# Seven block products in place of eight: six pairs of the first feed forward, nine pairs of the MLP

## The chip, the cores and the metric

The kernel runs on one core of a Trainium2 chip. The metric is the device time of one execution in microseconds (us); several runs are made and their median is taken. Beside the times there is one profiled execution, whose rows are shown below.

The engines are TensorE (PE in the rows; its weight loads are PEld), VectorE (DVE), ScalarE (ACT), GpSimd (POOL) and SyncE (SP), which issues the DMAs. Each of them works through its own queue in order. TensorE writes its results to PSUM, which holds eight banks of 128 x 512 float32 numbers; all other tiles lie in SBUF.

## What is computed

Two transformer blocks in a row on one sequence of 256 tokens with 1024 features, in float32. The first block has a mixer of three attention branches, an attention to a memory, and a gated feed forward; the second has modulation rows computed from a vector `c`, a mixer of forgetting attention and retention, and an MLP. The two parts that the change touches, cut to their core:

```python
# first block: D_FF = 2816
a = u @ w_in                                        # 1024 -> 2 * D_FF
h = h + (silu(a[..., :D_FF]) * a[..., D_FF:]) @ w_out
# second block: D_FF_2 = 4096
u = square(relu(h @ w_mlp_in))
x = x + gate_f * (u @ w_mlp_out)
```

## The kernel before

**Operands in two parts.** Each float32 operand is split into a high part that TensorE takes as fp32r and a low part, the rest. `mm3` makes one product out of three matmuls: high by high, low by high, high by low. The weights are split as they are used: a DMA brings a tile `raw` of 128 x 1024, ScalarE copies it into the high part `wh`, VectorE subtracts to get the low part `wl` (`cols`).

**A planner writes the order.** `Plan` records every operation; a list scheduler then gives each engine its order and each tile its slot before anything runs. An operation's key is its latest start by the planner's own costs, or its earliest start plus a margin (8 us in most entries) if that comes first. Among operations that can start, the smaller key goes first. `TUNING` holds one entry of parameters for each 140 dense matmuls (`WINDOW`) in the order they are issued, some with extra leads for named chains. The dense matmuls themselves keep the order of the program. SBUF tiles come from pools of slots: 37 of 4 KB (`k4`), 14 of 2 KB (`k2`), 12 of 1 KB; PSUM has eight slots (`ps`). A DMA may be placed up to 30 us (`HORIZON`) ahead of its need, if a slot is free.

**The first feed forward (`swiglu`, `ffn`).** The hidden width is cut into 11 pairs of 128 rows. For each pair, `up` makes two products with transposed output (`dense_T`): `aa` for the silu half and `bb` for the other, 48 matmuls of 256 columns each, one PSUM bank each. `glu` applies silu on ScalarE, multiplies on VectorE, and splits the product into the pair's hidden tile `hT`. `out_steps` multiplies `hT` by the rows of `w_ffn_out` into five accumulators (`out_accs`: two of 512 columns for token tile 0; 512, 256 and 256 for tile 1), which stay in PSUM for the whole stage. So three banks are left for `up`. The last six steps (`LAG1`) are done for token tile 0 first and then for tile 1, so that the norm of tile 0 starts early. `between` starts parts of the modulation: each part is four DMAs of `w_ada_2` tiles and four multiply-and-sum instructions on VectorE (`mod_part`); `MODF` lists the pairs after which one is started.

**The MLP (`mlp`).** 16 pairs, the last two (`TAIL`) plain as above. For the other 14 a pair's product with `w_mlp_out` is a 2 x 2 block product: two token tiles by two row blocks, and two row blocks by two halves of 512 columns. Plain, that is eight block products of three matmuls, 24 matmuls of 512 columns. For the pairs listed in `FASTM` a scheme with seven block products (`FAST`) is used: 21 matmuls, and in exchange sums of blocks, made on VectorE: of the activations in `pair_sums`, of the weights in `pair_weights`. The results are kept as seven accumulators in seven PSUM banks for the whole stage, plain pairs (`PLAIN`) adding into the same seven; `pair_end` combines them at the end and adds them to `x`. One bank is left for `up`. A pair's product is made two pairs after its `up`.

Of the kernel before, what the change touches and what calls it, by code (L numbers as in the profile page):

```python
# [15 lines left out]
AF = mybir.ActivationFunctionType  # L16
ALU = mybir.AluOpType
# [3 lines left out]
P = 128  # L21
S = 256
NT = 2
DM = 1024
KT = 8
D_FF = 2816
# [78 lines left out]
FFN = [2] * 11  # L105
# [531 lines left out]
class Net:  # L637
# [1012 lines left out]
    def swiglu(self, u, done):  # L1650
        nc, flow = self.nc, self.flow
        mods = []

        def swi(t, ac):
            sl = self.k(1, [P, S], nm="silu")
            nc.scalar.activation(sl, ac[:, :S], AF.Silu)
            yield
            nc.vector.tensor_tensor(sl, ac[:, S:], sl, ALU.mult)
            yield
            return sl  # L1660

        def glu(hT, aa, bb, n):
            sl = self.k(2, [P, n, S], nm="silu")
            nc.scalar.activation(sl, aa, AF.Silu)
            yield
            nc.vector.tensor_tensor(sl, bb, sl, ALU.mult)
            yield
            self.split(hT[0][0], hT[1][0], sl)
            yield

        def up(k0, n):
            hT = self.hidden(n)
            if k0 == 0:
                return hT, self.first_up(hT, u, n, [("w_ffn_in", 0), ("w_ffn_in", D_FF)], swi)
            aa, = self.dense_T(u, self.cols("w_ffn_in", k0 * P, (k0 + n) * P), n * P)
            bb, = self.dense_T(u, self.cols("w_ffn_in", D_FF + k0 * P, D_FF + (k0 + n) * P), n * P)
            return hT, [flow.start(glu(hT, aa, bb, n), "glu")]

        def between(i):
            if i in MODF:  # L1680
                self.next_part()
            if i == 9:
                self.scale, self.shift, self.gain = self.mod(1), self.mod(0), self.gain_row(self.a["norm_final"])

        self.ffn("ffn", FFN, "w_ffn_out", up, done, LAG1, between)


    def modulation(self):
# [525 lines left out]
        self.out_steps(self.out_accs(), [(hT, k, 2 * tail + k) for k in range(2 * TAIL)], w_out, True, done, 3)  # L2214

LAG1, LAG2 = 6, 6
TAIL, FASTM = 2, (2, 4, 6, 8, 10, 12, 13)
MODF = (0, 2, 4, 5, 6, 7)
MODG = ((4, 0), (4, 1), (1, 0), (5, 0))


def build(tc, a, out):
    with ExitStack() as ctx:
        e = ctx.enter_context
        n = Net(a)
        nc, flow = n.flow, n.flow
        x = n.fixed(NT * DM, "x").rearrange("p (t n) -> p t n", t=NT)
        for t in range(NT):
            nc.lead = LEADS[3 + t]
            for c in range(0, DM, 512):  # L2230
                nc.sync.dma_start(x[:, t, c:c + 512], a["x"][t * P:(t + 1) * P, c:c + 512])
        nc.lead = 0.0
        n.setup()
        u, mem = n.mixer(x)
        u = n.memory_attention(x, u, mem)
        late = {}

        def end_ffn(t, acs):
            if t == 0:
                late["u"] = n.act_pair()  # L2240
                late["chain"] = n.block2_norm(x, late["u"], n.gain)
            n.norms[t] = flow.start(late["chain"](t, acs), "b2norm")

        n.swiglu(u, end_ffn)

        def end_mix(t, acs):
            if t == 0:
                late["u2"] = n.act_pair()
            n.norms[t] = flow.start(n.resume(x, t, acs, late["u2"], (n.scale2, n.shift2), n.gate), "mlpnorm")

        n.block2_mix(x, late["u"], end_mix)
        n.x = x
        ends = []

        def end(t, acs):
            ends.append(flow.start(n.resume(x, t, acs, gate=n.gate, store=out)))

        n.mlp(late["u2"], end)
        flow.need(*ends)
        flow.need(*flow.waiting)  # L2260
        flow.schedule()
        wk, ps = e(tc.tile_pool(name="wk", bufs=1)), e(tc.tile_pool(name="ps", bufs=1, space=PSUM))
        dram = e(tc.tile_pool(name="dram", bufs=1, space=bass.MemoryType.DRAM))

        def place(r):
            if r.kind == "ps":
                return ps.tile([P, 512], F32, tag=f"ps{r.slot}", name=r.name)
            if r.kind == "dram":
                return dram.tile([P, r.n], r.dtype, name=r.name)
            return wk.tile([P, r.n], r.dtype, tag=r.name if r.kind == "fixed" else f"{r.kind}_{r.slot}", name=r.name)  # L2270

        flow.issue(tc, place)
# [42 lines left out]
```

## Time and profile before

| | us |
|---|---|
| median of 3 runs (757.82 to 758.5) | 757.98 |
| the profiled execution | 758.92 |
| its span, first to last instruction | 757.1 |
| TensorE busy in the span | 740.1 (98%) |
| VectorE busy | 611.9 (81%) |
| ScalarE busy | 420.3 (56%) |

The busy time of TensorE counts matmuls with modelled ends, which overlap; how fast it works is read from the starts of the matmuls in the timeline. Rows name tiles by the program's names without their numbers; nearly all operations are issued through one helper, so that their line is L634.

### The profile page before, as it was taken

The numbers are of one execution on the slowest core, as the hardware profiler recorded it, in microseconds if no ns is written. First come the engines' busy times: TensorE is split into PE (matmuls) and PEld (weight loads), VectorE is DVE, ScalarE is ACT, GpSimd is POOL, SyncE is SP. The second block draws the span as 40 slices with busy tenths as digits, with TensorE's granted clock in tenths as the row PEclk, the third lists the DMA queues.
The fourth block names the chain that finished last, engine by engine and source line by source line (L and its number), as shares of the span: only waits on it lengthen the run. The fifth ranks groups of instructions, "written<-read, shape, count | busy, mean of one in ns | idle before, by whom it ended". The sixth has DMA issues, their size and how long they took to land.

```text
span 757.1 us, 13129 instructions
## 1 busy us (share of the span) xinstructions
PE 740.1 (98%) x5090; PEld 671.9 (89%) x5090; DVE 611.9 (81%) x1026; ACT 420.3 (56%) x701; POOL 39.9 (5%) x50
## 2 busy tenths in 40 slices
PE   7999999999998999999999899999999999999998
PEld 4978999999897999999999788898887989998996
DVE  5999989798699995877455788888669879898857
ACT  6684875456287644344354555753546746767640
POOL 0012000010000000000000222020101000000000
PEclk9999999999999999999999999999999999999999
DMA  9828476976375797888877476545455487755521
GB/s 316 287 85 256 144 249 234 389 275 214 129 268 182 237 313 232 310 308 299 279 266 182 147 162 155 150 120 186 164 166 170 137 271 267 268 193 196 196 84 56
DMA packets 94931, 161.69 MB, mean 214 GB/s; under 512 B 8011, under 2 KB 58347, under 8 KB 94868
## 3 DMA queue, kind: packets, MB, share of 16 engines
q1 hardware_dynamic: 94868, 160.85, 65.3%
q8 instruction: 40, 0.66, 0.4%
q14 instruction: 23, 0.19, 0.1%
HBM read 159.75 MB, written 1.08 MB: 212 GB/s over the span
## 4 chain that ended last, share of the span: by engine, by line
PE 74%; DVE 13%; issue 6%; ACT 3%; DMA 3%; POOL 1%; SPq 0%; POOLq 0%; DVEq 0%; ACTq 0%
PE ps L634 74%; DVE wl L634 3%; DMA raw<-in_w_in_dram 2%; DVE x L634 1%; DVE s L634 1%; DVE xn L634 1%; DVE sc L634 1%; ACT wh L634 1%; DVE sum L634 1%; DVE gt L634 0%; SPq L634 0%; POOL s L634 0%; DVE mk L634 0%; DMA row<-in_norm_mix_dram 0%; ACT prob L634 0%
## 5 line engine op out<-in xcount | busy, mean ns | idle before, releaser
L634 DVE TENSOR_TENSOR wl<-raw,wh 128x1024 fp32r<-128x1024 f32 (+4 forms) x237 | 278.6, 1204 | 42.0 <-ACT wh L634 34.1
L634 PE MATMUL ps<-aT,wh 128*128 128x256 f32 x1664 | 305.8, 283 | 0.0
L634 ACT ACTIVATE wh<-raw 128x1024 fp32r<-128x1024 f32 (+4 forms) x237 | 241.9, 1040 | 106.3 <-DMA raw<-in_w_ffn_in_dram 24.2
L634 PEld LDWEIGHTS ps<-aT,wh 128*128 128x128 f32 x1664 | 258.4, 189 | 1.9 <-issue 0.4
L634 PE MATMUL ps<-aT,wl 128*128 128x256 f32 x832 | 235.9, 284 | 0.0
L634 PE MATMUL ps<-wh,aT 128*128 128x512 f32 (+5 forms) x672 | 182.2, 357 | 2.1 <-ACT wh L634 1.3
L634 PEld LDWEIGHTS ps<-aT,wl 128*128 128x128 f32 x832 | 157.1, 189 | 0.1
L634 PEld LDWEIGHTS ps<-wh,aT 128*128 128x128 f32 x672 | 118.8, 190 | 19.1 <-ACT wh L634 1.9
L634 PE MATMUL ps<-wl,aT 128*128 128x512 f32 (+5 forms) x336 | 117.5, 354 | 0.0
L634 PEld LDWEIGHTS ps<-wl,aT 128*128 128x128 f32 x336 | 63.6, 190 | 7.1
L634 PE MATMUL ps<-wh,hT 128*128 128x512 f32 (+1 forms) x260 | 67.6, 348 | 0.0
L634 DVE SCALAR_TENSOR_TENSOR raw<-raw,mod_c 128x1024 f32<-128x1024 f32 x48 | 57.3, 1219 | 8.0 <-DMA raw<-in_w_ada_dram 7.8
L634 PEld LDWEIGHTS ps<-wh,hT 128*128 128x128 f32 x260 | 45.3, 188 | 6.9
L634 PE MATMUL ps<-wl,hT 128*128 128x512 f32 (+1 forms) x130 | 45.2, 348 | 0.0
L634 PE MATMUL ps<-wh,blockl 128*128 128x512 f32 x105 | 41.4, 394 | 0.0
L634 PE MATMUL ps<-wh,blockh 128*128 128x512 f32 x105 | 41.4, 394 | 0.0
L634 PE MATMUL ps<-wl,blockh 128*128 128x512 f32 x105 | 41.4, 394 | 0.0
L634 POOL TENSOR_TENSOR s<-s,mhalf 128x1 f32<-128x1 f32 (+3 forms) x22 | 23.5, 1072 | 298.0 <-DVE s L634 297.8
L634 ACT ACTIVATE junk<-x 128x512 f32<-128x512 f32 (+1 forms) x29 | 16.1, 555 | 38.7 <-DVE x L634 36.4
L634 PEld LDWEIGHTS ps<-wl,hT 128*128 128x128 f32 x130 | 24.5, 188 | 3.4
L634 ACT ACTIVATE prob<-ps,s 128x256 f32<-128x256 f32 (+1 forms) x48 | 20.0, 447 | 9.4 <-DVE s L634 9.3
L634 ACT ACTIVATE aT<-ps 128x256 fp32r<-128x256 f32 (+1 forms) x41 | 17.7, 459 | 11.1 <-PE ps L634 10.7
(300 smaller groups left out, 807.2 us busy)
## 6 DMA issues: line engine op xcount, KB each, us to landing
raw<-in_w_in_dram SPq DMA_DIRECT2D x62, 512.0 KB, 6.0
raw<-in_w_ada_dram SPq DMA_DIRECT2D x48, 512.0 KB, 6.0
raw<-in_w_ffn_in_dram SPq DMA_DIRECT2D x44, 512.0 KB, 5.9
raw<-in_w_mlp_in_dram SPq DMA_DIRECT2D x32, 512.0 KB, 4.2
raw<-in_w_mlp_out_dram SPq DMA_DIRECT2D x32, 512.0 KB, 5.3
raw<-in_w_ffn_out_dram SPq DMA_DIRECT2D x22, 512.0 KB, 5.2
raw<-in_w_out_dram SPq DMA_DIRECT2D x16, 512.0 KB, 4.5
raw<-in_w_up_dram SPq DMA_DIRECT2D x6, 512.0 KB, 5.3
```

The lines of the kernel that those rows point to most:

```text
L634: getattr(get[o.eng], name)(*map(real, args), **{k: real(v) for k, v in kw.items()})
```

## The change

The first feed forward gets the structure of the MLP. `ps` are seven accumulators. Pairs 2 to 7 use the seven products, pairs 0 and 1 the eight, and the last three pairs (`TAILF`) are plain, through `out_steps`. A pair's product comes two pairs after its `up` (`LATE`), and is cut in two: four block products stand between the two halves of the next `up`, the other three or four behind it. The silu product is now written into a page of blocks. The modulation parts are started after pairs 3 to 8 in place of 0, 2, 4, 5, 6 and 7. In the MLP, pairs 3 and 9 join `FASTM`. `n.x = x` only moves up, since `pair_end` is now used earlier. The diff, cut to its core:

```diff
-        def glu(hT, aa, bb, n):
-            sl = self.k(2, [P, n, S], nm="silu")
-            nc.scalar.activation(sl, aa, AF.Silu)
-            yield
-            nc.vector.tensor_tensor(sl, bb, sl, ALU.mult)
-            yield
-            self.split(hT[0][0], hT[1][0], sl)
-            yield
-
-        def up(k0, n):
-            hT = self.hidden(n)
-            if k0 == 0:
-                return hT, self.first_up(hT, u, n, [("w_ffn_in", 0), ("w_ffn_in", D_FF)], swi)
-            aa, = self.dense_T(u, self.cols("w_ffn_in", k0 * P, (k0 + n) * P), n * P)
-            bb, = self.dense_T(u, self.cols("w_ffn_in", D_FF + k0 * P, D_FF + (k0 + n) * P), n * P)
-            return hT, [flow.start(glu(hT, aa, bb, n), "glu")]
+        x, w_in, w_out, n = self.x, "w_ffn_in", "w_ffn_out", D_FF // S
+        tail = n - TAILF
+        blocks, pages, chains = {}, {}, {}
+        hT, ps = self.act_pair(), [self.acc() for _ in range(7)]
+
+        def first(t, ac):
+
+            o = yield from swi(t, ac)
+            pt, = yield from self.bank()
+            for j in range(2):
+                self.tr(pt[:, j * P:(j + 1) * P], o[:, j * P:(j + 1) * P])
+            self.pair_place(pages[0], pt[:, :S], t)
+            yield
+
+        def sums(p, *before):
+            yield from flow.after({0: list(before)})
+            blocks[p] = yield from self.pair_sums(pages[p], p in FASTF)
+
+        def silu(p, sl, ac):
+            nc.scalar.activation(sl, ac, AF.Silu)
+            yield
+
+        def glu(p, sl, ac):
+            yield from flow.after({0: chains["a", p]})
+            if p >= tail:
+                nc.vector.tensor_tensor(sl, ac, sl, ALU.mult)
+                yield
+                c, k = divmod(2 * (p - tail), 4)
+                self.split(*(e[c][:, k:k + 2, :] for e in hT), sl)
+                yield
+                return
+            pages[p] = self.pair_page()
+            flat = "p a b -> p (a b)"
+            nc.vector.tensor_tensor(pages[p][:, 0:4, :].rearrange(flat), ac.rearrange(flat), sl.rearrange(flat), ALU.mult)
+            yield
+            yield from sums(p)
+
+        def up(p, part, fn, sl):
+            c0 = part * D_FF + p * S
+            ac, = self.dense_T(u, self.cols(w_in, c0, c0 + S), S)
+            chains["ab"[part], p] = flow.start(fn(p, sl, ac), "glu")
+
+        begun = set()
+
+        def down(p, which, w):
+            flow.need(chains["b", p])
+            self.pair_product(ps, blocks[p], w, begun, p == tail - 1, which)
...
-        self.ffn("ffn", FFN, "w_ffn_out", up, done, LAG1, between)
+        self.main("ffn")
+        pages[0] = self.pair_page()
+        wf = [self.held(w_in, c, c + S) for c in (0, D_FF)]
+        firsts = []
+        for t in range(NT):
+            flow.need(self.norms[t])
+            ac = self.acc()
+            for i in range(2):
+                self.dense_t(u, t, wf[i], ac[:, i * S:(i + 1) * S])
+            firsts.append(flow.start(first(t, ac), f"first_{t}"))
+        chains["b", 0] = flow.start(sums(0, *firsts), "glu")
+        between(0)
+        for p in range(1, n + LATE):
+            sl = self.k(2, [P, 2, S], nm="silu")
+            q = p - LATE
+            w = self.pair_weights(w_out, 2 * q, q in FASTF) if 0 <= q < tail else None
+            if p < n:
+                self.main("ffn")
+                up(p, 0, silu, sl)
+            if w:
+                down(q, slice(0, 4), w)
+            if p < n:
+                up(p, 1, glu, sl)
+            if w:
+                down(q, slice(4, 8), w)
+            if p < n:
+                between(p)
+        flow.need(flow.start(self.pair_end(ps, x), "ffnsum"))
+        flow.need(*[chains["b", p] for p in range(tail, n)])
+        self.out_steps(self.out_accs(), [(hT, k, 2 * tail + k) for k in range(2 * TAILF)], w_out, True, done, LAG1)
...
-TAIL, FASTM = 2, (2, 4, 6, 8, 10, 12, 13)
-MODF = (0, 2, 4, 5, 6, 7)
+TAIL, TAILF, LATE, FASTF, FASTM = 2, 3, 2, (2, 3, 4, 5, 6, 7), (2, 3, 4, 6, 8, 9, 10, 12, 13)
+MODF = (3, 4, 5, 6, 7, 8)
```

## Rows read from the trace of the kernel before

**Rows 1.** The chain that ended last, feed forward and MLP: start us, us, what.

```profile
243.60 181.42 PE ps L634 x1345
...
576.97 164.67 PE ps L634 x1045
```

**Rows 2.** Busy us by engine in four stretches, then granted clock, DMA share, GB/s.

```profile
243.60:425.00 181.40, 181.40 (x1347) 172.77 (x1348) 125.51 (x153) 80.40 (x95) 1.16 (x2) 1.00 0.80 260
577.00:741.70 164.70, 164.70 (x1046) 148.54 (x1047) 137.86 (x196) 104.60 (x142) 0.00 (x0) 1.00 0.58 198
632.00:648.00 16.00, 16.00 (x109) 14.72 (x108) 15.72 (x27) 8.53 (x13) 0.00 (x0) 1.00 0.94 328
424.00:440.00 16.00, 14.02 (x77) 11.07 (x76) 14.60 (x32) 11.57 (x25) 4.00 (x4) 0.89 0.56 167
```

**Rows 3.** Timeline of TensorE, matmuls of 256 and 512 columns: start us, us.

```profile
305.31 0.40 PE L634 MATMUL ps<-aT,wh 128*128 128x256 f32 x2
...
316.24 0.39 PE L634 MATMUL ps<-aT,wh 128*128 128x256 f32 x2
...
726.69 0.40 PE L634 MATMUL ps<-wh,blockh 128*128 128x512 f32 x1
...
729.49 0.39 PE L634 MATMUL ps<-wh,blockh 128*128 128x512 f32 x1
```

**Rows 4.** Groups of VectorE in the feed forward (248 to 424 us) by shape.

```profile
L634 DVE TENSOR_TENSOR wl<-raw,wh 128x1024 fp32r<-128x1024 f32 x62 | 75.2, 1222 | 32.2 <-ACT wh L634 24.6 <-PE ps L634 6.8
L634 DVE SCALAR_TENSOR_TENSOR raw<-raw,mod_c 128x1024 f32<-128x1024 f32 x24 | 28.7, 1218 | 2.3 <-DMA raw<-in_w_ada_dram 2.2
```

**Rows 5.** Groups of VectorE in the MLP (584 to 736 us) by shape.

```profile
L634 DVE TENSOR_TENSOR sums<-raw,raw 128x512 f32<-128x512 f32 x14 | 9.6, 688 | 2.7 <-DMA raw<-in_w_mlp_out_dram 2.5
L634 DVE TENSOR_TENSOR wl<-sums,wh 128x1024 fp32r<-128x1024 f32 x7 | 8.5, 1217 | 0.0
L634 DVE TENSOR_TENSOR blocks<-blocks 128x128 f32<-128x128 f32 x28 | 6.8, 283 | 0.1
...
L634 DVE TENSOR_TENSOR blockl<-blocks,blockh 128x384 fp32r<-128x384 f32 x7 | 3.8, 549 | 0.0
```

**Rows 6.** Timeline of VectorE, instructions that follow on one another.

```profile
257.99 4.62 DVE L634 TENSOR_TENSOR wl<-raw,wh 128x1024 fp32r<-128x1024 f32 x4
...
741.09 0.68 DVE L634 TENSOR_TENSOR sum<-sum,modrow 128x512 f32<-128x512 f32 x1
741.69 0.68 DVE L634 TENSOR_TENSOR sum<-ps,sum 128x512 f32<-128x512 f32 x1
```

**Rows 7.** Timeline of TensorE, the last matmul of two `bb` banks.

```profile
299.63 0.28 PE L634 MATMUL ps<-aT,wl 128*128 128x256 f32 x1
...
384.02 0.28 PE L634 MATMUL ps<-aT,wl 128*128 128x256 f32 x1
```

**Rows 8.** Timeline of VectorE, the products that empty these two banks.

```profile
299.95 0.69 DVE L634 TENSOR_TENSOR silu<-ps,silu 128x512 f32<-128x512 f32 x1 [2.90 <-PE ps L634]
...
386.84 0.68 DVE L634 TENSOR_TENSOR silu<-ps,silu 128x512 f32<-128x512 f32 x1
```

**Rows 9.** Timeline of ScalarE: a late silu of the feed forward, a late relu.

```profile
381.87 0.58 ACT L634 ACTIVATE silu<-ps 128x512 f32<-128x512 f32 x1
...
728.90 0.58 ACT L634 ACTIVATE relu<-ps 128x512 f32<-128x512 f32 x1
```

**Rows 10.** Instructions by tile: the weight DMAs' first and last start, their landing, last uses.

```profile
L634 SPq DMA_DIRECT2D raw<-in_w_ffn_in_dram x44: 367/378/1089, 203.9 to 378.7; - x44
...
L634 DVE TENSOR_TENSOR silu<-ps,silu x12: 414/692/692, 250.1 to 412.6; 128x512 f32<-128x512 f32 x10, 128x256 f32<-128x256 f32 x2
...
L634 SPq DMA_DIRECT2D raw<-in_w_mlp_in_dram x32: 367/379/660, 542.5 to 707.9; - x32
...
DMA to landing us min/median/max: 3.3/4.2/8.9
...
L634 ACT ACTIVATE relu<-ps x16: 569/598/602, 585.4 to 737.5; 128x512 f32<-128x512 f32 x16
```

More of the change, by code (lines that the diff above doesn't have):

```diff
@@ L2232, in build @@
         nc.lead = 0.0
+        n.x = x
         n.setup()
@@ L2251, in build @@
         n.block2_mix(x, late["u"], end_mix)
-        n.x = x
         ends = []
```

## The prediction

> **What bounds the kernel now.** I read the chain that ended last first. In both stages that change it is TensorE alone: one unbroken piece of 1345 matmuls over 181.4 us of the feed forward and one of 1045 over 164.7 us of the MLP [rows 1]. The reader is to see that no other engine has a link in either piece: there time goes only if TensorE has less to do, and comes back only if something makes it wait. [...] The timeline of TensorE gives its pace by starts: 93 matmuls of 256 columns in 10.93 us, 0.1175 us each, and 12 of 512 in 2.80 us, 0.233 us each [rows 3]. (The durations in the rows overlap and are no pace.)
>
> **What the change removes.** A pair with seven block products has 21 matmuls for 24: 3 x 0.233 = 0.70 us. Six pairs of the feed forward and two more of the MLP: 8 x 0.70 = 5.6 us. In the feed forward the eight block pairs also lose the cut of token tile 1 into 512, 256 and 256 columns: six times 2 x 0.1175 - 0.233 = 0.002 us a pair, 0.1 us in all. So 5.7 us of TensorE, 4.3 of them in the feed forward. All of it is on the path, since nothing else is in the chain.
>
> **What it adds on VectorE.** A turn of the loop in the middle (turns 4 to 9, with a fast pair and a modulation part each) holds: four splits of up weights, two of down weights, four weight sums of 512, the splits of the two sum tiles (1024 and 512), four block sums of 128, block splits of 512 and 384, the silu product of 512, and four modulation sums of 1024. Instructions that follow on one another start closer than their durations: four of 1024 in 4.62 us, 1.155 us each, against 1.222 in the group; those of 512 start 0.60 us apart against 0.68 [rows 4, 6]. The lag between two is hidden by about 0.07 to 0.08, so I put 384 at 0.47 and 128 at 0.20 (groups: 0.549 and 0.283) [rows 5]. The turn: 4.62 + 2.31 + 2.40 + 1.76 + 0.80 + 1.07 + 0.60 + 4.62 = 18.2 us. TensorE needs 96 x 0.1175 + 21 x 0.233 = 16.2 us. VectorE is therefore the slower engine in these six turns, by 2.0 us each, 12 us in all.
>
> What hides that is the lead with which weights are fetched. The last up tile of the MLP is issued at 707.9 and used by the last 24 matmuls before the relu at 737.5, from 734.4 on: 26.5 us; less landing (4.2 us) and the two split instructions, about 20 us of finished work. In the feed forward the last one leads by some 31 us (378.7; used 2.8 us before 412.6) [rows 10]. After the change the feed forward holds tiles as the MLP does now (pages and blocks of up to three pairs, six to eight weight pages for a fast pair), so I take the MLP's 20 us. 12 is less than 20, turns 1 to 3 are light, and the MLP stretch at 98% [rows 2] did not stop TensorE: cost nothing, bounds nothing to 2 us (durations in place of starts: 19.9 us a turn, 22 us in six turns, 2 more than 20). If the cover is gone, each turn costs its whole excess of 2.0 to 3.7 us. In the MLP two more pairs become fast, some 4.7 us of VectorE each; 137.9 + 9.4 = 147 of 163 us, still covered.
>
> [...]
>
> **What it adds in PSUM.** The feed forward had five accumulators and three banks for `up`; now seven and one. Each of the two products of an `up` must be emptied while the block products behind it run: 12 matmuls, 2.8 us, behind the silu half; nine, 2.1 us, behind the other half of a fast pair. From the start of the last matmul into the bank that leaves 2.9 and 2.2 us. Behind a bank that is late stands the whole queue of TensorE.
>
> How late is it today, with nothing hanging on it? The second half is mostly emptied at once: last matmul at 299.63, VectorE's product ends at 300.64, 1.0 us. So in nine of ten pairs; once it took 3.5 us (384.02 to 387.52, behind a split) [rows 7, 8]. The first half is looser: going back 48 matmuls from 384.02, its last one started at 378.4, and the silu ended at 382.45, 4.1 us later [rows 7, 9]. Over pairs 2 to 10 I find about 0.9 us five times, and 2.1, 2.6, 3.5 and 4.1. The MLP empties its one bank by a relu in 0.7 to 1.4 us twelve times and in 2.8 to 2.9 us three times of 15, as at 728.90 (ends 2.8 us after the pair's products began at 726.69) [rows 3, 9]; behind it stand 4.9 us of products, so it never showed.
>
> With 0.25 us for TensorE to notice (an estimate from the 0.32 us between 299.63 and VectorE's start at 299.95 [rows 7, 8]): first half, 3.5 and 4.1 would stop TensorE 0.8 and 1.4 us, 0.25 us a pair; by the MLP's relu 0.04; I take 0.2. Second half: 3.5 stops it 1.55 us in one of ten, 0.16 a pair. Eight pairs: 8 x 0.36 = 2.9 us. Bounds: nothing, if the planner, which knows the eight slots, empties them in time as in the MLP; 8 x (1.4 + 1.55) = 24 us if every bank is as late as the worst. I take 2.9 since most are prompt.
>
> **What it moves.** `pair_end` is eleven VectorE instructions, 11 x 0.60 = 6.6 us [rows 6], behind the last block product. Turn 10 follows with 96 matmuls, 11.3 us, and needs one bank at once and a second 5.6 us later, when the first of the seven is long free: cost nothing; without that turn, up to 6.6 us. The tail of three plain pairs with the two token tiles one after the other is as before. The modulation parts move past the first pairs; their rows are needed after the stage, their DMAs are the same 24, and SP issues nothing new: nothing. The planner's entries count matmuls: 66 fewer in the feed forward shift all later entries by half a window, so the leads for the projections behind it fall on other operations. The nearest row is that transition, where TensorE is idle 2.0 of 16 us [rows 2]: from 2 us gained to 2 us lost; I take nothing.
>
> **Sum.** -5.7 + 2.9 = -2.8 us. The profiled execution took 758.9 us, so 756.1; the median of the runs stands 0.9 us below it: 755.2 us, faster by 0.4%. About 0.2%, 1.5 us, is what a measurement here can tell from no change.
>
> **The rivals.**
> *The whole saving arrives* (752.3 us). For it: the MLP with one spare bank and a nearly full VectorE shows no pause. Against: its products behind a bank last 4.9 us, here 2.8 and 2.1.
> *One bank is too few* (757 to 759.4 us, the same). If hand-overs cost twice what I take, 5.8 us, the saving is gone. For it: VectorE has less slack in these turns than when the one late product in ten was counted. It decides from 0.5 us a pair on. [...]
> *VectorE becomes the bound* (slower). Its groups waited 32 us before 62 splits, about 0.5 us each [rows 4]; if six splits a turn keep that wait while VectorE is behind, a turn takes 18.2 + 3.1 = 21.3 us, 5.1 over TensorE's; six turns are 31 us, 11 beyond the lead of 20. -5.7 + 2.9 + 11 = +8, 766 us. It decides from 16.2 + 20 / 6 = 19.5 us a turn on. Against: most of that wait was for work not yet there, and the 98% stretch [rows 2] has next to none.
> *The later stages lose by the shifted entries* (2 us lost, with 4.5 us of hand-overs: 758.8; 4 us lost: 760.8).
>
> **How the numbers follow.** My forecast, 753.5 to 756.4 us, 0.42; the whole saving, 751 to 753.5, 0.20; one bank too few, 756.5 to 759.5, 0.18; VectorE the bound, 0.12; later stages lose beyond the bound, 0.08. Faster 0.62, same 0.18, slower 0.20. The likeliest case's own range is 753.5 to 756.4. The range that leaves two in ten out is 751.6 to 760.0: the whole saving with a little from the shift at one end, mild forms of the slower cases at the other.
>
> **What would show it.** Right: the feed forward's piece of TensorE about 177 to 180 us long with a few gaps under 1.6 us, each behind a silu or its product; starts still 0.1175 and 0.233 us apart; the MLP's piece 1.4 us shorter without gaps; VectorE near 95% in the middle of the feed forward. Wrong: gaps in TensorE's weight loads that end with `wl`, growing from turn 4 to 9 (VectorE the bound); gaps of a microsecond at every hand-over (one bank too few); both pieces shorter by their full share and the time not (the stages behind).

## The result and the profile after

| | before | after |
|---|---|---|
| median of 4 runs each, us | 758.10 (757.82 to 758.50) | 753.66 (752.07 to 754.89) |
| ratio, 95% interval | | 0.9939 [0.9927, 0.9952] |
| the profiled execution, us | 758.92 | 754.89 |
| its span, us | 757.1 | 753.1 |

The change makes the kernel 4.4 us (0.6%) faster. The forecast was 755.2; the measured time lies at the lower edge of the likeliest case (753.5 to 756.4). The profiled executions of the kernel after, of e6 and of e9 are the slowest among the runs of each (754.89, 759.65 and 762.40 us).

The chain that ended last, of the kernel after, answers to [rows 1]: start us, us, what.

```profile
375.79 12.11 DMA raw<-in_w_ffn_in_dram
387.98 1.06 ACT wh L634
389.04 0.49 ACT silu L634
389.57 31.93 PE ps L634 x207
...
424.08 2.23 DVE wl L634
427.10 0.90 DVE xn L634
...
574.67 162.95 PE ps L634 x1039
```

The MLP is still one piece of TensorE, 1.7 us shorter. The feed forward is no longer one: the chain enters TensorE at 389.57 from a silu, that from a weight split on ScalarE, and that from a DMA that took 12.11 us. And where the feed forward ends, the chain now passes through VectorE (`wl`, then `xn`).

The feed forward and the MLP as in [rows 2], and two stretches from the middle of the feed forward, of the kernel after: us; busy us of PE, PEld, DVE, ACT, POOL; granted clock, DMA share, GB/s.

```profile
243.20:424.70 181.50, 180.27 (x1308) 169.94 (x1308) 165.22 (x238) 93.99 (x122) 2.43 (x3) 1.00 0.78 263
574.70:737.60 162.90, 162.90 (x1040) 146.91 (x1041) 146.75 (x213) 107.81 (x146) 0.00 (x0) 1.00 0.58 200
...
320.00:360.00 40.00, 40.00 (x290) 37.63 (x289) 39.83 (x61) 21.60 (x26) 0.00 (x0) 1.00 0.88 296
360.00:390.00 30.00, 28.77 (x203) 26.60 (x203) 29.97 (x43) 15.27 (x20) 0.00 (x0) 1.00 0.93 332
```

VectorE went from 125.5 to 165.2 us in the feed forward and is busy 99.6% and 99.9% of two stretches in a row; TensorE still paused only once there. The engine at 99.9% is not what it paused for, as the timelines of TensorE and ScalarE show around that pause:

```profile
387.71 0.40 PE L634 MATMUL ps<-wh,blockl 128*128 128x512 f32 x1
387.94 0.40 PE L634 MATMUL ps<-wl,blockh 128*128 128x512 f32 x1
389.57 0.50 PE L634 MATMUL ps<-aT,wh 128*128 128x256 f32 x2 [1.23 <-ACT silu L634]
```
```profile
386.47 1.06 ACT L634 ACTIVATE wh<-raw 128x1024 fp32r<-128x1024 f32 x1 [5.63 <-DMA raw<-in_w_ffn_in_dram]
387.98 1.06 ACT L634 ACTIVATE wh<-raw 128x1024 fp32r<-128x1024 f32 x1 [0.45 <-DMA raw<-in_w_ffn_in_dram]
388.94 0.58 ACT L634 ACTIVATE silu<-ps 128x512 f32<-128x512 f32 x1
```

The silu empties the one spare bank. It stands in ScalarE's queue behind two weight splits, the first of which waited 5.63 us for its tile. TensorE starts 1.4 us later than its pace of 0.23 us would have had it. A place like this, where a bank is emptied while block products run and TensorE then goes on with the next half of an `up`, is a hand-over. The stage has 16, and the other 15 came in time: at 14 of them the silu or the product ended 0.9 to 1.6 us after the start of the bank's last matmul, and at the last, where the product ended 3.8 us after it, TensorE had already gone on in another bank.

Only eleven of the 16 test a single spare bank. The eight plain block products (`PLAIN`) add into four accumulators, not into all seven as the description of the kernel says, and the planner gives a tile its bank at its first use. The other three accumulators take theirs in the first half of pair 2's product, so the four hand-overs before that had banks to spare; the last one had accumulators that were already read out. e6 below shows the second spare bank.

The group of these splits in the kernel after, and the landing of the up weights, beside 5.9 us median and 9.4 at most before:

```profile
L634 ACT ACTIVATE wh<-raw 128x1024 fp32r<-128x1024 f32 x58 | 60.4, 1054 | 30.6 <-DMA raw<-in_w_ffn_in_dram 13.7 <-PE ps L634 6.5 <-DVE raw L634 5.3
```
```profile
DMA to landing us min/median/max: 3.5/7.0/12.1
```

Where the 4.0 us of the two spans went, from the starts of matmuls in the two timelines. FFN is the feed forward's first to last matmul, the gap that from there to the first matmul of the next projection (proj2); the MLP is counted up to its last block product, and 15.2 us follow in both kernels:

| us | before the FFN | FFN | gap | proj2 to MLP | MLP |
|---|---|---|---|---|---|
| before | 243.80 | 185.18 | 1.42 | 144.28 | 167.25 |
| after | 243.24 | 182.22 | 3.07 | 143.82 | 165.56 |
| difference | -0.56 | -2.96 | +1.65 | -0.46 | -1.69 |

So -4.3 + 1.4 in the feed forward, and 1.65 us given back right behind it. The 0.56 us ahead of the feed forward are spread between executions: in e1 below, the same kernel, it starts at 243.98.

### The profile page after: what moved, and what is told of

The parts are those of the page before. It is cut to its first block, busy times and chain, and to the rows that moved or that the text cites. A ratio compares the mean times of both kernels' runs of the same rounds, so it can differ in the third digit from the quotient of the medians.

```text
span 753.1 us, 13107 instructions
## 1 busy us (share of the span) xinstructions
PE 734.9 (98%) x5018; PEld 665.4 (88%) x5018; DVE 659.0 (88%) x1125; ACT 435.7 (58%) x727; POOL 36.4 (5%) x49
## 3 DMA queue, kind: packets, MB, share of 16 engines
HBM read 159.75 MB, written 1.08 MB: 214 GB/s over the span
## 4 chain that ended last, share of the span: by engine, by line
PE 42%; DVE 5%; DMA 2%; issue 1%; ACT 1%; POOLq 0%; POOL 0%; SPq 0%; DVEq 0%; ACTq 0%
PE ps L634 42%; DMA raw<-in_w_ffn_in_dram 2%; DVE x L634 1%; DVE wl L634 1%; DVE raw L634 1%; DVE sum L634 1%; DVE gt L634 1%; DVE xn L634 0%; ACT wh L634 0%; DVE mixed L634 0%; DVE gg L634 0%; DVE sums L634 0%; POOLq L2371 0%; ACT sq L634 0%; DVE aT L634 0%
## 5 line engine op out<-in xcount | busy, mean ns | idle before, releaser
L634 PE MATMUL ps<-wh,aT 128*128 128x512 f32 (+5 forms) x732 | 199.0, 357 | 1.5 <-ACT wh L634 0.8
L634 PE MATMUL ps<-wh,blockl 128*128 128x512 f32 x161 | 63.5, 394 | 0.0
L634 PE MATMUL ps<-wl,blockh 128*128 128x512 f32 x161 | 63.3, 393 | 0.0
L634 PE MATMUL ps<-wh,blockh 128*128 128x512 f32 x161 | 63.1, 394 | 0.0
L634 ACT ACTIVATE blockh<-blocks 128x512 fp32r<-128x512 f32 (+2 forms) x44 | 24.0, 557 | 24.9 <-DVE blocks L634 24.4
L634 PEld LDWEIGHTS ps<-wl,blockh 128*128 128x128 f32 x161 | 30.3, 188 | 7.1
L634 PEld LDWEIGHTS ps<-wh,blockl 128*128 128x128 f32 x161 | 30.2, 188 | 5.8
L634 PEld LDWEIGHTS ps<-wh,blockh 128*128 128x128 f32 x161 | 30.2, 188 | 5.8
L634 ACT ACTIVATE wh<-sums 128x1024 fp32r<-128x1024 f32 (+1 forms) x30 | 25.1, 837 | 13.2 <-DVE sums L634 12.8
L634 DVE TENSOR_TENSOR wl<-sums,wh 128x1024 fp32r<-128x1024 f32 (+1 forms) x30 | 28.6, 954 | 2.8 <-ACT wh L634 2.8
```

The lines of the kernel that those rows point to most:

```text
L634: getattr(get[o.eng], name)(*map(real, args), **{k: real(v) for k, v in kw.items()})
```

## The experiments

The theory after the result: the saving of matmuls arrives in full; VectorE's nearly full queue delays the norm behind the feed forward by 1.65 us; the single pause is a hand-over. The rival for the 1.65 us: the planner's entries, which count matmuls and now fall on other operations. Kernels named e1 to e13 are edits of the kernel after unless said otherwise; for e5 (pair 2 alone fast in the feed forward) there is no time.

**e1, unchanged.**

> The changed kernel once more. My theory: the 5.7 us of matmuls come through in full, and what the profile shows lost beside them comes from VectorE, full from about 320 to 424 us: one hand-over of 1.4 us and a start of the next stage that is later by some 1.7 us. The first depends on when a DMA lands, so it may be absent or there twice: median 752.5 to 754.5 us, hand-over gaps of 0 to 3 us in the new trace. Rival (one spare bank as such): a gap at several hand-overs, and always at the same ones.

753.56 us (752.41 to 756.20, 6 runs), ratio 0.9945 [0.9931, 0.9958]. The pause at a hand-over is there at the same place, but 0.3 us long in this profile; the gap before proj2 is 3.17 us. Every engine has the same instructions in the same order as in the first profile of this kernel, so the length of the pause goes by when the tile lands (11.4 us at most here, 12.1 there); the gap is much the same in both.

**e2, the MLP's part alone**, an edit of the kernel before.

```diff
-TAIL, FASTM = 2, (2, 4, 6, 8, 10, 12, 13)
+TAIL, FASTM = 2, (2, 3, 4, 6, 8, 9, 10, 12, 13)
```

> The kernel before with pairs 3 and 9 of the MLP fast, nothing else. If two times 0.70 us of matmuls are all that counts there: 1.4 us under the kernel before, about 756.7 us, the MLP's piece of TensorE without gaps. Rival (VectorE, with 4.7 us more for each pair, stops TensorE): no gain, 757.5 us or more, with gaps that end with a weight split.

756.59 us (755.55 to 757.13, 11 runs), ratio 0.9980 [0.9971, 0.9988]: 1.43 us less than the 758.02 of before beside it. The two pairs bring their 2 x 0.70 us in full.

**e3, the feed forward's part alone.**

```diff
-TAIL, TAILF, LATE, FASTF, FASTM = 2, 3, 2, (2, 3, 4, 5, 6, 7), (2, 3, 4, 6, 8, 9, 10, 12, 13)
+TAIL, TAILF, LATE, FASTF, FASTM = 2, 3, 2, (2, 3, 4, 5, 6, 7), (2, 4, 6, 8, 10, 12, 13)
```

> The changed kernel with the MLP's old list of fast pairs. If the parts add up: 1.4 us over the changed kernel, about 755.1 us, 3 us under the kernel before. Rival (the MLP gives back what it saves): as the changed kernel, within 0.5 us.

754.96 us (754.78 to 755.83, 5 runs), ratio 0.9965 [0.9952, 0.9977]: -3.1 us. With e2's 1.4 that is -4.5 for -4.4 measured: the two parts add up, and it is the feed forward's part, with the gap behind it, that got less than its 4.3.

**e4, the modulation parts early**, which frees VectorE at the end of the feed forward.

```diff
-MODF = (3, 4, 5, 6, 7, 8)
+MODF = (0, 1, 2, 3, 4, 5)
```

> The changed kernel with the modulation parts after pairs 0 to 5 in place of 3 to 8: the same work on VectorE, 13.9 us of it some three turns earlier, when VectorE was busy 21.4 of 32 us. My theory (VectorE's backlog at the end of the stage makes the late hand-over and the late start behind it): both shrink, 1.5 to 3 us under the changed kernel, 750.7 to 752.2 us, and VectorE below 90% from 390 to 424 us. Rival (the planner's shifted entries make the late start): the hand-over may go, the start stays, at most 1.4 us gained. Rival (the lead is taken from the front instead): no gain, gaps in the first turns.

755.61 us (755.04 to 756.37, 6 runs), ratio 0.9970 [0.9959, 0.9981], 2 us worse than after. A stretch of e4, and the worst of three pauses in its timeline of TensorE:

```profile
390.00:424.00 34.00, 34.00 (x228) 31.17 (x227) 25.37 (x37) 16.50 (x24) 1.66 (x2) 1.00 0.64 170
```
```profile
364.28 0.50 PE L634 MATMUL ps<-aT,wh 128*128 128x256 f32 x2 [0.82 <-DVE blocks L634]
```

At the end of the stage VectorE is now busy 25.4 of 34 us, and proj2 still starts 3.08 us after the feed forward. VectorE's backlog is therefore not what makes proj2 late: this part of the theory falls. What its profile shows of the loss are pauses at three hand-overs, 2.2 us together, for 1.4 in the kernel after and 0.3 in e1. At one of them the silu stood behind a split that had waited 2.79 us for its tile. At the other two (364.28 and 381.94) the product stood on VectorE behind more than 7 us of splits and weight sums without a pause: no late tile right ahead, but a queue of work.

**e8, the entries put back** in front of the matmuls that they were made for.

```diff
-(i + 1) * WINDOW)
+(i + 1) * WINDOW - 66 * (i >= 17))
```

> The changed kernel with the planner's entries from the 17th on ending 66 matmuls earlier, so that the stages behind the feed forward meet the entries that they had before. If the shifted entries make the next stage start late: some 1.7 us under the changed kernel, 752 us. My theory (VectorE's backlog does): within 0.8 us of the changed kernel.

753.00 us (751.04 to 753.40, 4 runs), ratio 0.9927 [0.9911, 0.9944]. The gap before proj2 goes from 3.07 to 1.37 us. The norm's steps on VectorE and the transposes behind them, in the kernel after and then in e8:

```profile
424.00 2.31 DVE L634 TENSOR_TENSOR wl<-raw,wh 128x1024 fp32r<-128x1024 f32 x1
...
427.02 0.98 DVE L634 SCALAR_TENSOR_TENSOR xn<-xn,s,modrow 128x512 f32<-128x512 f32 x1
...
428.14 0.63 PE L634 MATMUL ps<-ident,xn 128*128 128x128 f32 x4 [1.97 <-DVE xn L634]
```
```profile
423.91 1.65 DVE L634 SCALAR_TENSOR_TENSOR xn<-xn,s,modrow 128x512 f32<-128x512 f32 x1
...
425.51 1.04 PE L634 MATMUL ps<-ident,xn 128*128 128x128 f32 x8
```

After the change the planner puts a weight split ahead of the norm's last `xn`; it took 2.31 us, where such a split takes 1.22, while GpSimd worked from 423.93 to 425.22. With the entries back no split stands there, and `xn` comes 3.1 us earlier. The rival was right. The medians show less than the gap: 753.00 for 753.66, with overlapping ranges, since proj2 to MLP takes 144.29 us for 143.82, so 1.2 us net in the profiles; and the pause, at the same place in the same order, was 1.8 us long in this one.

**e6, the cut of the block products undone**: all of them behind the second half of `up`.

```diff
             if p < n:
                 up(p, 0, silu, sl)
-            if w:
-                down(q, slice(0, 4), w)
             if p < n:
                 up(p, 1, glu, sl)
             if w:
-                down(q, slice(4, 8), w)
+                down(q, slice(0, 8), w)
```

> The changed kernel with all block products of a pair behind the second half of the up, none between the halves. The first half's bank then has no cover: silu ends 0.9 us after the last matmul's start, with 0.25 us for TensorE to notice and 0.12 for the matmul itself about 1.05 us of gap in each of eight turns, 8.4 us, less what the slack gives back at the end of the stage (up to 3 us): 5 to 9 us over the changed kernel, 759 to 763 us. Rival (the cut does nothing, the planner has another bank in time): within 1 us of the changed kernel.

757.47 us (755.46 to 759.65, 10 runs), ratio 0.9995 [0.9984, 1.0007]: 3.8 us worse than after, less than what I expected. The timeline of TensorE in e6:

```profile
320.62 0.39 PE L634 MATMUL ps<-wh,blockh 128*128 128x512 f32 x1
...
321.54 0.40 PE L634 MATMUL ps<-wh,blockl 128*128 128x512 f32 x1
322.22 0.51 PE L634 MATMUL ps<-aT,wh 128*128 128x256 f32 x2 [0.28 <-ACT silu L634]
```

Five matmuls of block products stand between the halves although the program has none there. In the other four pairs that come after a fast pair's sums 9, 5, 5 and 5 do. In the turns of pairs 2 to 4 none do, and TensorE still goes on without a pause: there the second half follows the first at its pace of 0.12 us, as at 270.72, while the silu that empties the first runs from 270.92 to 271.52. So a second spare bank is there. The planner moves products of different accumulators past one another, so the sentence in the description of the kernel before, that the dense matmuls keep the order of the program, holds only for matmuls that depend on one another. By the starts of matmuls three of these five hand-overs are late, by 0.45, 0.36 and 1.26 us: the feed forward takes 183.52 us, 1.3 more than in the kernel after. The rest of the loss lies behind it: the gap before proj2 is 5.16 us and proj2 to MLP takes 145.54, and again a weight split, of 2.23 us, stands ahead of the norm's `xn`. So e6 bears little on the hand-overs: five matmuls (1.2 us) behind a bank were enough in two of four cases.

**e7, 14.4 us more of VectorE work**: four of the weight sums of each fast pair of the feed forward are made again with the same values, 24 x 0.60 us.

```diff
             tt(w2[:, hi], w1[:, hi], w0[:, hi], ALU.subtract)
+            if w == "w_ffn_out":
+                for _ in range(2):
+                    tt(w2[:, hi], w1[:, hi], w0[:, hi], ALU.subtract)
...
```

> The changed kernel with the four weight sums of each fast pair of the feed forward made twice (the same values written again): 6 x 4 x 0.60 = 14.4 us more on VectorE, nothing else. By the prediction's count a middle turn then takes 20.6 us of VectorE for 16.2 of TensorE, over the 19.5 from which VectorE decides: 6 x 4.4 = 26 us behind, 20 of them covered, so 6 us or more over the changed kernel, 760 to 766 us, with gaps that end with a weight split. Rival (VectorE still has room, 165 of 181 us): under 2 us more.

767.94 us (766.64 to 769.27, 4 runs), ratio 1.0133 [1.0118, 1.0148]: 14.3 us over after for 14.4 us of work. Two stretches of e7 and the largest pause of TensorE in them, with another of 1.99 us behind it:

```profile
320.00:360.00 40.00, 39.17 (x273) 35.91 (x272) 39.44 (x60) 20.79 (x25) 0.00 (x0) 1.00 0.89 303
360.00:390.00 30.00, 24.88 (x159) 22.47 (x157) 29.71 (x47) 11.22 (x14) 0.00 (x0) 0.89 0.80 277
```
```profile
369.77 0.79 PE L634 MATMUL ps<-wh,blockh 128*128 128x512 f32 x1 [3.83 <-ACT wh L634]
```

Of the 14.4 us nothing was hidden: the feed forward takes 193.24 us, 11.0 more than in the kernel after, and the gap behind it 6.74, 3.7 more. The pauses end with ScalarE's splits (`wh`) of weights for the block products. The granted clock fell too (0.89 in the second stretch), which could have made a part of the loss; but from 320 to 434 us VectorE was busy 111.25 of 114 us, so the stage could not have ended much sooner at full clock. In the kernel after, VectorE thus has no reserve left; that one more fast pair would have cost its whole VectorE work is my estimate from this.

**e9, two fast pairs in place of six.** Four times 0.70 us more for TensorE, some 20 us less for VectorE, nine or twelve matmuls behind each half as before.

```diff
-TAIL, TAILF, LATE, FASTF, FASTM = 2, 3, 2, (2, 3, 4, 5, 6, 7), (2, 3, 4, 6, 8, 9, 10, 12, 13)
+TAIL, TAILF, LATE, FASTF, FASTM = 2, 3, 2, (2, 7), (2, 3, 4, 6, 8, 9, 10, 12, 13)
```

> The changed kernel with pairs 2 and 7 alone fast in the feed forward: the same seven accumulators and one spare bank, 4 x 0.70 = 2.8 us more matmuls, some 22 us less on VectorE. If a full VectorE makes the late hand-over: no gap at a hand-over; the later start of the next stage stays, since the planner's entries make it. 753.6 + 2.8 - 0.3 to 1.4 = 755 to 756.1 us. Rival (one spare bank as such): the gap at turn 9 stays, 756.4 us or more.

760.22 us (759.49 to 762.40, 5 runs), ratio 1.0032 [1.0019, 1.0045]. This is a miss of 4 us: with a lighter VectorE I expected hand-overs at least as prompt. A stretch of e9, its group of up and down weight splits on ScalarE, and the timelines of ScalarE and VectorE ahead of two pauses of TensorE:

```profile
320.00:360.00 40.00, 39.11 (x275) 36.15 (x274) 33.35 (x45) 16.90 (x20) 0.00 (x0) 1.00 0.90 311
```
```profile
L634 ACT ACTIVATE wh<-raw 128x1024 fp32r<-128x1024 f32 x58 | 60.1, 1053 | 52.8 <-DMA raw<-in_w_ffn_in_dram 46.6 <-DMA raw<-in_w_ffn_out_dram 3.0 <-PE ps L634 1.4
```
```profile
312.86 1.06 ACT L634 ACTIVATE wh<-raw 128x1024 fp32r<-128x1024 f32 x1 [6.25 <-DMA raw<-in_w_ffn_in_dram]
```
```profile
313.96 1.23 DVE L634 TENSOR_TENSOR wl<-raw,wh 128x1024 fp32r<-128x1024 f32 x1 [0.33 <-ACT wh L634]
315.10 0.68 DVE L634 TENSOR_TENSOR blocks<-ps,silu 128x512 f32<-128x512 f32 x1
...
367.61 0.69 DVE L634 TENSOR_TENSOR sums<-raw,raw 128x512 f32<-128x512 f32 x1 [2.70 <-DMA raw<-in_w_ffn_out_dram]
368.22 0.68 DVE L634 TENSOR_TENSOR blocks<-ps,silu 128x512 f32<-128x512 f32 x1
```
```profile
315.84 0.51 PE L634 MATMUL ps<-aT,wh 128*128 128x256 f32 x2 [0.26 <-DVE blocks L634]
...
368.96 0.51 PE L634 MATMUL ps<-aT,wh 128*128 128x256 f32 x2 [1.08 <-DVE blocks L634]
```

VectorE idles 17% of that stretch, yet four hand-overs are late and the feed forward takes 187.42 us. At each of the four, the product that empties the bank stood in VectorE's queue behind an operation on a weight tile that had come late: twice a split that waited for ScalarE's copy of such a tile (the copies at 312.86 and 329.38, after waits of 6.25 and 6.56 us), once a weight sum, once a modulation sum. ScalarE waited 46.6 us for up weights, against 13.7 in the kernel after. That gave the next theory: not VectorE's load but late DMAs at the head of a queue make hand-overs late. (It does not cover e4, where ScalarE waited 13.4 us for up weights and two of three pauses had VectorE's own work ahead of the product.)

**e12, e9 with a quarter of the modulation's DMA bytes.**

```diff
-            nc.sync.dma_start(raw, self.mod_w[i, :, j, :])
+            nc.sync.dma_start(raw[:, 0:256], self.mod_w[i, :, j, 0:256])
...
+            for c in range(4):
+                nc.vector.scalar_tensor_tensor(raw[:, 256:512], raw[:, 0:256], 1.0, self.mod_c[:, c * 256:c * 256 + 256], ALU.mult, ALU.mult,
```

> Two fast pairs as in e9 (760.2 us), and each of the 24 modulation DMAs brings only the first 256 of its 1024 columns (0.13 MB for 0.52 MB, 9.4 MB less in the feed forward); VectorE multiplies and sums these four times over, so that it works about as long as before and three quarters of the modulation weights are left out. Theory (e9's late hand-overs come from weight tiles that land late because the queue and the DMA engines are full): landings of the up weights go back towards 5 us, ScalarE's wait for them from 46 us to under 20, at least three of the four gaps at hand-overs go (3 of some 5 us), and the time is 756 to 758. Rival (the fixed order that the planner wrote for pairs 2 and 7 is what is late, whatever the DMAs do): the gaps stay, 759.5 to 761.

758.34 us (757.52 to 758.77, 11 runs), ratio 1.0004 [0.9995, 1.0013]. The same stretch and the same group in e12:

```profile
320.00:360.00 40.00, 40.00 (x285) 37.41 (x285) 37.17 (x120) 17.57 (x21) 0.00 (x0) 1.00 0.72 226
```
```profile
L634 ACT ACTIVATE wh<-raw 128x1024 fp32r<-128x1024 f32 x58 | 59.6, 1053 | 30.5 <-DMA raw<-in_w_ffn_out_dram 9.2 <-DMA raw<-in_w_ffn_in_dram 8.9 <-DVE wl L634 4.7
```

The median landing of an up weight falls from 6.8 to 4.9 us, ScalarE's wait for them from 46.6 to 8.9, all four pauses are gone, and the feed forward takes 182.90 us, 4.5 less than in e9, though VectorE is busier than there. The profiles show this, but not that the bytes alone did it: with four VectorE instructions in place of each modulation sum, the planner also ordered VectorE, ScalarE and the DMAs anew. The time came down by 1.9 us between the medians (on two chips; before stood at 758.09 and 757.74) and lies 0.3 above the theory's range, since proj2 to MLP took 145.80 us, 2 more than in the kernel after.

**e13, e9 with the entries of e8.**

```diff
-(i + 1) * WINDOW)
+(i + 1) * WINDOW - 66 * (i >= 17))
```

> Two fast pairs as in e9, with the planner's entries behind the feed forward shifted back by the same 66 matmuls as in e8 (54 would be exact here). Theory (e9 lost about 2 us behind the feed forward to the shifted entries and the rest, some 5 us, to hand-overs inside it): proj2 starts 1.4 us after the feed forward in place of 3.1, the feed forward stays at about 187.4, and the time is 757.5 to 759. Rival (entries shifted by 54 are not what made proj2 late in e9): 759.5 to 761.

757.52 us (756.18 to 760.21, 11 runs), ratio 0.9994 [0.9984, 1.0004]. The gap is 1.37 us again for 3.12 and proj2 to MLP 144.42 for 145.42: the shifted entries cost e9 2.7 us behind the feed forward. The feed forward itself took 185.57 with one hand-over late by 1.6 us and one by 0.2, where I had expected it unchanged at four late ones, 3.0 us together. Yet until past the last hand-over every engine has the same instructions in the same order as in e9. So in one order such pauses come and go from execution to execution, with the landings; ScalarE's wait for up weights was 39.0 us here, for 46.6.

**e11, half of the weight sums on GpSimd**, on top of e8, to relieve VectorE.

```diff
-            tt(w2[:, hi], w1[:, hi], w0[:, hi], ALU.subtract)
+            (nc.gpsimd.tensor_tensor if w == "w_ffn_out" else tt)(w2[:, hi], w1[:, hi], w0[:, hi], ALU.subtract)
...
-            tt(w3, w1[:, lo], w2[:, lo], ALU.subtract)
+            (nc.gpsimd.tensor_tensor if w == "w_ffn_out" else tt)(w3, w1[:, lo], w2[:, lo], ALU.subtract)
```

> The kernel with aligned entries, with two of the four weight sums of each fast pair of the feed forward on GpSimd, which is busy 5% of the span: 12 x 0.60 = 7.2 us less on VectorE, 12 x 1.3 us more on GpSimd (its only 512-column sum in the trace took 1.30 us). If VectorE's fullness costs more than the one hand-over: 1 to 2 us under the aligned kernel, 751 to 752 us. Rival (the stage is TensorE's again and only the DMA's landing matters): within 0.7 us of it. Rival (the two engines slow each other, or the longer chain comes late): slower than it by more than 0.7 us.

762.87 us (761.86 to 763.63, 5 runs), ratio 1.0060 [1.0048, 1.0073], 10 us worse than e8. Groups of GpSimd in e11, and the timelines of TensorE and VectorE at its longest pause:

```profile
L634 POOL TENSOR_TENSOR sums<-raw,sums 128x512 f32<-128x512 f32 x6 | 13.3, 2217 | 16.0 <-DVE sums L634 16.0
L634 POOL TENSOR_TENSOR sums<-raw,raw 128x512 f32<-128x512 f32 x6 | 10.2, 1699 | 105.1 <-DMA raw<-in_w_ffn_out_dram 92.6 <-PE ps L634 12.4
```
```profile
352.27 0.64 PE L634 MATMUL ps<-aT,wh 128*128 128x256 f32 x2 [2.23 <-DVE blocks L634]
```
```profile
350.39 1.21 DVE L634 SCALAR_TENSOR_TENSOR raw<-raw,mod_c 128x1024 f32<-128x1024 f32 x1
351.54 0.68 DVE L634 TENSOR_TENSOR blocks<-ps,silu 128x512 f32<-128x512 f32 x1
```

GpSimd takes 1.70 and 2.22 us for a sum. At three of the five late hand-overs the product stood right behind a modulation sum on VectorE, at two behind a split: the list for VectorE was another one, with the emptying product further back. VectorE was not relieved either. Its group of weight splits in the feed forward (243 to 424 us), in e11 and then in e8:

```profile
L634 DVE TENSOR_TENSOR wl<-raw,wh 128x1024 fp32r<-128x1024 f32 x64 | 85.1, 1356 | 6.5 <-ACT wh L634 6.4
```
```profile
L634 DVE TENSOR_TENSOR wl<-raw,wh 128x1024 fp32r<-128x1024 f32 x64 | 76.3, 1222 | 2.9 <-ACT wh L634 2.9
```

That is 8.8 us more, where 12 sums of 0.60 us were taken away. Nine of these splits started while a GpSimd sum ran, and eight of the nine took 2.3 us in place of 1.22. So of the second rival, that the two engines slow each other, VectorE's side is shown, and e11 does not test whether a lighter VectorE helps. How much of the 10 us is this and how much the order stays open.

**e10, e8 with the modulation parts one turn earlier**, so that the last one's DMAs don't meet the last up weights.

```diff
-MODF = (3, 4, 5, 6, 7, 8)
+MODF = (2, 3, 4, 5, 6, 7)
```

> The kernel with aligned entries, with the modulation parts after pairs 2 to 7 in place of 3 to 8, so that the last four of their DMAs are no longer issued right before the weights of turn 9, which took 12 us to land. If that landing makes the late hand-over: no gap at turn 9, 1 to 1.8 us under the aligned kernel (753.0), about 751.6 us. Rival (the lead is taken from the turns before, as with the parts after pairs 0 to 5): 753 us or more, with gaps between 360 and 385 us.

752.56 us (751.84 to 753.03, 5 runs), ratio 0.9926 [0.9912, 0.9940]. Its feed forward is one piece of the chain again, at 243.58, and the stretch of the old pause is full:

```profile
243.58 177.10 PE ps L634 x1279
```
```profile
360.00:390.00 30.00, 30.00 (x216) 28.16 (x216) 28.45 (x41) 15.55 (x20) 0.00 (x0) 1.00 0.91 297
```

First to last matmul it is 180.88 us: 185.18 less the whole 4.3. The landings are not what changed: up weights still take 6.7 us in the median and 11.2 at most, and ScalarE still waits 14.7 us for them. The silu now stands ahead of the late tile's split, as ScalarE's timeline shows where the pause was:

```profile
386.79 0.60 ACT L634 ACTIVATE silu<-ps 128x512 f32<-128x512 f32 x1 [4.59 <-PE ps L634]
...
388.19 1.06 ACT L634 ACTIVATE wh<-raw 128x1024 fp32r<-128x1024 f32 x1 [0.28 <-DMA raw<-in_w_ffn_in_dram]
```

It beats both kernels, the kernel after by 1.1 us between medians (their ranges overlap: 752.07 to 754.89 there); against e8 alone the difference is within the spread.

## Why the prediction came out as it did

**What TensorE saves (-5.7 us): right.** The parts alone brought 1.4 (e2) and, without the pause, 4.3 (e10's feed forward); matmuls of block products still start 0.23 us apart, as at 387.71 and 387.94.

**VectorE, 18.2 us a turn behind a lead of 20 us, costed at nothing: the number was right, its reason was not.** No pause in the kernel after ends with `wl`. But a reserve of 20 - 12 = 8 us should have hidden more than half of e7's 14.4 us, and hid none. The step that fails is taking the MLP's lead for the feed forward's. Counted in the same way in the kernel after, the last up tile is issued at 381.6 and used by the 24 matmuls from 405.9 on: 24.3 us, less two split instructions and a landing of 7.0 us in the median and up to 12.1 (I subtracted 4.2 [rows 10]), leaves 10 to 15 us in place of 20. That is about the 12 us that were needed, and VectorE, busy 39.83 of 40 and 29.97 of 30 us, has no slack in these stretches. The rival in which VectorE becomes the bound was thus nearer than 0.12 said: 2.4 us a turn more, as in e7, and it is there. The 24 sums of e7 cost 14.3 us, near their count by starts (24 x 0.60 = 14.4) and not by durations (24 x 0.688 = 16.5).

**The hand-overs (+2.9 us): the mechanism was right, the size was half or less.** One pause of 1.4 us in the kernel after, and at the same place in the same order 0.3 in e1, 0.5 in e3 and 1.8 in e8; none in e10. I carried the lateness of before over to each of eight pairs as 0.36 us. But eleven hand-overs, not 16, had a single spare bank, and ten of these eleven were prompt. That the planner, which knows the slots, kept them prompt is likely and not tested. What remained in the kernel after is ScalarE standing before a weight tile that has not landed, with the silu behind it: the longest landing was 12.1 us there and 11.4, 11.4 and 12.4 in e1, e3 and e8, in step with the pauses; e10 puts the silu first and has none. That VectorE's load plays no part is not shown: in e4 and e11 the product stood behind VectorE's own work. One spare bank in place of three did not hurt by itself: nine or twelve matmuls behind it, 2.1 or 2.8 us, hid every prompt emptying of 0.9 to 1.6 us.

**The shifted entries (0, bounds 2 us either way): the size was wrong, the bounds held.** They cost 1.65 us at the gap and gave 0.46 back in the stage after it. e8 undoes the first.

**`pair_end` and the moved modulation parts (0).** No pause stands at `pair_end`. The moved parts were not free: one turn earlier and the pause is gone from the profile (e10 beside e8), three turns earlier and the kernel loses 2 us (e4).

Together: 5.7 - 1.4 - 1.2 = 3.1 us by the terms; the spans differ by 4.0. The rest is 0.56 us ahead of the feed forward, where no operation changed, and 0.3 us in the MLP. The likeliest case held with its hand-overs halved, and most of what that gave (1.5 us) went to the shift (1.2). That these two misses nearly cancel is luck, and that VectorE's work just fitted is luck as well. Left open: why proj2 to MLP takes 1.6 and 2.0 us longer in e9 and e12 than in the kernel after (e13 puts 1.0 of e9's down to the entries), and what part of e11's loss is the order.

## What to carry to other kernels

When a stage runs on one spare bank, look at what stands ahead of the emptying operation in its engine's queue: an operation on a tile that a DMA still has to bring (TensorE idle for 1.23 us in the kernel after, for 1.08 in e9), or a run of that engine's own work (0.82 us in e4, 2.23 in e11). The busy share alone did not tell: from 320 to 360 us VectorE had a late hand-over at 83% in e9, and none at 99.6% in the kernel after. Before counting on a lead that covers a nearly full engine, add work to that engine and see whether the time moves: here it moved 14.3 us for 14.4 (e7), although no pause had been put down to VectorE. Where a schedule is tied to a count of operations, a change of the count moves every later entry, and the next stage has to be read as well.

## What the hardware showed that was not expected

The DMA of an up weight's tile (512 KB) took 5.9 us to land in the median before and 7.0 after, with 12.1 at most in a stretch in which the DMA share was 0.93 at 332 GB/s; the median was 6.8 in e9 and 4.9 in e12, with 9.4 MB less in the stage.

A weight split on VectorE that started while GpSimd worked on two tiles of 512 columns took 2.3 us in place of 1.22: in eight of nine cases in e11, and at 424.00 in the kernel after. In the ninth case the split took 1.22 us and GpSimd's sum 2.50, the longest of its kind. Beside GpSimd's instructions on 1 and 8 columns a split took 1.23 and 1.22 us (at 157.90 and 447.56 in the kernel after).

TensorE's clock fell behind the feed forward. Three stretches of 4 us there in the kernel after:

```profile
424.40:428.40 4.00, 2.03 (x19) 1.82 (x18) 4.00 (x6) 3.29 (x11) 1.55 (x2) 1.00 0.84 200
428.40:432.40 4.00, 2.70 (x11) 1.47 (x10) 3.81 (x12) 2.88 (x5) 1.39 (x2) 0.73 1.04 306
432.40:436.40 4.00, 4.00 (x13) 3.24 (x13) 3.59 (x8) 3.35 (x6) 0.00 (x0) 0.50 0.82 252
```

TensorE was busy 2.03 and 2.70 of 4 us in the first two, and its granted clock was 0.73 in the second stretch and 0.50 in the third; matmuls of 512 columns started 0.43 us apart there (434.86 and 435.29), for 0.233 at a granted clock of 1.00. In e8, busy 3.37 and 2.70 us in the first two stretches, it kept 1.00 from 424.40 to 440.40. The kernel before, with a gap of 1.42 us, lost some clock too: 0.82 and 0.76 from 432 to 436 and 440. So the length of the gap is not shown to be the cause. What this is worth by itself no run separates: the whole of e8 is 0.66 us between medians.
